# A list of five named buffers for the gathered expert rows, apart from the ring of the expert tiles

## The chip, the cores and the metric

One core of a Trainium2 chip runs the whole program. The metric is the device time of one execution in microseconds (us). The kernel is written in Python against a layer that keeps tiles in named buffers, puts in the semaphores between engines and sets each engine's order of instructions itself.

## The reference

The reference is two transformer blocks in float32 on one sequence of 256 tokens of width 2048. The first has a gated linear attention and a SwiGLU layer; the second a hybrid of sparse and stick-breaking attention, a memory attention, and a PEER layer, which is where the change lies. PEER keeps 16384 experts; expert e is a row `u[e]` and a row `v[e]` of 2048 numbers each. Each of 8 heads scores two sets of 128 keys against the token's query, keeps the best 16 pairs of keys (a pair names one expert) and softmaxes their scores to gates. Written out for one token x, with the 128 chosen experts e and their gates g:

```python
y = sum(g[e] * gelu(dot(u[e], x)) * v[e] for e in chosen)
out = rmsnorm(h + y, norm_final)
```

## The kernel before, in words

All activations lie with the width on the partitions. Up to the queries of PEER the kernel is a row of linear layers in three-pass float32, with weights loaded ahead, split into a high and a low part in buffers with the tags wh and wl, and multiplied on TensorE. The change touches nothing of that part but shares its buffers: `wtile(tag, i)` (line 188) gives the one buffer `tag` + `i`, a tile of 128 x 2048 floats, 1 MB. For the PEER layer there are wr0 to wr2, wh0 to wh2 and wl0 to wl2.

PEER is computed in two ways at once. For 160 of the 256 tokens (ND) the kernel multiplies with all 16384 experts and sets the gate of every expert that wasn't chosen to zero. For the other 96 tokens (SETS, 64 and 32) it fetches only the chosen rows.

The dense way reads the whole of u and v as 256 tiles of 1 MB, in the order of `expert_order` (line 77). They go through a ring of four buffers: wr0, wr1 and wr2, and ("wl", 2), which is appended at line 1307. `load_raw` (line 1035) takes a free slot and issues the next tile's load on SP (line 1041); `raw_weight` (line 1045) gives the slot of the last used tile back, loads ahead, and hands out the next tile. So SP is up to three tiles ahead of TensorE. `u_pair` (line 1071) takes two tiles of u and makes 256 hidden units for 160 tokens; between the pairs of the first part `gates` (line 1361) builds the dense gates with matmuls of one-hot rows that VectorE writes in `gates_rows` (line 1351). The loop at line 1392 takes the tiles of v.

The sparse way gathers. One gather fetches 128 rows of 2048 numbers, 1 MB, with an indirect DMA that POOL issues (line 1130). There are 192: 96 of u (64 for the first set, 32 for the second), then 96 of v. Gathered rows of u are multiplied and summed by VectorE at line 1142 into `hs`, rows of v are multiplied by `hs` and added to `hn` at line 1150. `gathered_steps` (line 1135) starts the first NG = 5 gathers; each step then uses one gather's rows and starts the gather five places on. The steps are paced by the ring: `raw_weight` adds 0.83 to a credit for each tile and takes a step for each whole one, and each gather waits for the matmul that was written last before it (line 1132). So there are about 83 gathers for 100 tiles, until all 192 are through.

Which buffer a gather uses is decided in `gather` (line 1126). Python reads `n % NG // 2` from the left, as (n % NG) // 2, while the tag alternates with n:

```python
g = fetched[n] = wtile(("wh", "wl")[n % 2], n % NG // 2, F32R).bitcast(F32)
```

For n from 0 to 9 that is wh0, wl0, wh1, wl1, wh2, wl0, wh0, wl1, wh1, wl2, and then from the start.

The layer underneath lets an instruction that reuses a buffer wait until the buffer's last user is done, and may place it later in its engine's order than the code does. An engine and SP's queue take their instructions in order.

Of the kernel before, what the change touches and what calls it, by code (L numbers as in the profile page):

```python
# [9 lines left out]
F32 = mybir.dt.float32  # L10
F32R = mybir.dt.float32r
# [21 lines left out]
LAG = 4  # L33
RATE = 3
PER = 1
NG = 5
SHARE = 5 / 8


# [42 lines left out]
def build(tc, a, out, dbg=None):  # L82
# [4 lines left out]
    with es:  # L87
# [100 lines left out]
        def wtile(tag, i, dt=F32):  # L188
            pool = wp if i < 2 else st["ext"]
            return pool.tile([P, 2048], dt, name=tag, tag=f"{tag}{i}", bufs=1)  # L190
# [21 lines left out]
        def weight(kt, n, hold=False):  # L212

            if not hold:
                w_free.extend(i for i in st["held"] if i < st["nw"])
                st["held"] = []
            load_ahead()
            w, h, l, i = ready.pop(0)
            st["held"].append(i)
            assert w == kt * n, (w, kt, n)  # L220
            v = lambda t: t[:, :w].rearrange("p (k n) -> p k n", n=n)
            return v(h), v(l)
# [105 lines left out]
        with ExitStack() as e1:  # L328
# [22 lines left out]
            with ExitStack() as e2:  # L351
# [145 lines left out]
                wh, wl = weight(KT, 16)  # L497
# [87 lines left out]
        with ExitStack() as e1:  # L585
# [18 lines left out]
            with ExitStack() as e2:  # L604
# [183 lines left out]
                wh, wl = weight(KT, 24)  # L788
# [154 lines left out]
        with ExitStack() as e1:  # L943
# [43 lines left out]
            for j in range(8):  # L987
                mt = mp.tile([P, 2, T], F32, name="mt2", tag="mt2")
                nc.sync.dma_start(mt, a["memT"][:, 2 * j:2 * j + 2])
                for i in range(2):  # L990
                    k = 2 * j + i
                    g = gains[:, 4, k:k + 1]
# [15 lines left out]
            for n4 in range(4):  # L1008
                wh, wl = weight(16, P)
# [15 lines left out]
        with ExitStack() as e1:  # L1025
# [98 lines left out]
            fetched = {}  # L1124

            def gather(n):
                if n < len(plan):
                    t, d, m = plan[n]
                    g = fetched[n] = wtile(("wh", "wl")[n % 2], n % NG // 2, F32R).bitcast(F32)
                    ins = nc.gpsimd.indirect_dma_start(g, None, a[t], bass.IndirectOffsetOnAxis(ap=d["ix"][:, m:m + 1], axis=0))  # L1130

                    tc.add_manual_dep(ins.ins, last_pe[0], mybir.DependencyInfo(
                        mybir.DependencyClass.Sync, mybir.DependencyReason.DATA), reason="pace")

            def gathered_steps():
                for n in range(NG):
                    gather(n)
                yield True
                for n, (t, d, m) in enumerate(plan):
                    g, h = fetched.pop(n), d["hs"]  # L1140
                    if t == "u_rows":
                        nc.vector.tensor_tensor_reduce(out=g, in0=g, in1=d["hn"], scale=1.0, scalar=0.0, op0=ALU.mult, op1=ALU.add,  # L1142
                                                       accum_out=h[:, m:m + 1])
                        if m == d["w"] - 1:
                            nc.scalar.activation(h, h, AF.Gelu_apprx_tanh)
                            nc.vector.tensor_tensor(h, h, d["gs"], ALU.mult)
                    elif m == 0:
                        nc.vector.tensor_scalar(d["y"], g, h[:, 0:1], None, ALU.mult)
                    else:
                        nc.vector.scalar_tensor_tensor(d["y"], g, h[:, m:m + 1], d["y"], ALU.mult, ALU.add)  # L1150
                        d["done"] = m == d["w"] - 1
                    gather(n + NG)
                    yield True
# [363 lines left out]
```

## Time and profile before

| | us |
|---|---|
| median of 2 runs | 3147.11 (3143.66 to 3150.56) |
| the profiled execution | 3146.22 |
| its span, first to last instruction | 3144.1 |
| TensorE (PE) busy in it | 3006.3 |
| VectorE (DVE) busy | 1713.8 |

The span is what the profile covers; the rest of the profiled execution lies around it. "PE" is TensorE's matmuls, "POOL" GpSimd, "SPq" the queue of SP. "PEclk" is the granted clock of TensorE as a share of its full speed, "DMA share" the mean busy share of the core's 16 DMA engines. In a row of a wait, "A <- B" says that A waited and that B ended the wait. A name such as wl stands for all buffers of that tag. A busy TensorE isn't one at its peak, since matmuls overlap.

### The profile page before, as it was taken

Reading aid. Unit: us, or ns where it says so; the run is one execution under the profiler, and the core shown is the slowest. Engines: PE = TensorE matmul, PEld = TensorE weight load, DVE = VectorE, ACT = ScalarE, POOL = GpSimd, SP = SyncE. Lnnn points to the kernel's source line nnn. Section 1 sums busy time; section 2 is a strip of 40 time slices with the busy share of each in tenths; the row PEclk is TensorE's granted clock in tenths of the full one; section 3 lists DMA queues with packets and bytes.
Section 4 is the critical chain, followed back from the end, with each engine's and each line's share of the span. In section 5 each row is a group of like instructions: output and inputs, shape, how many; then the busy total and the mean of one; then the engine's idle time right before and its main releaser. Section 6 shows DMA issues by size and latency. Waiting matters only on the chain.

```text
span 3144.1 us, 52115 instructions
## 1 busy us (share of the span) xinstructions
PE 3006.3 (96%) x22786; PEld 2938.4 (93%) x22786; DVE 1713.8 (55%) x2300; ACT 870.3 (28%) x1074; POOL 538.8 (17%) x367
## 2 busy tenths in 40 slices
PE   8999999999999999999999999999989889989998
PEld 7989999999999999899998999998989889989988
DVE  6575665454545555455867885656544434344332
ACT  5335544333333444343655421111100000000001
POOL 1120012011020210000111531112222222332210
PEclk9999999999999999999999999999999989999999
DMA  5444455554555546545355559999999989999995
GB/s 191 170 147 150 160 206 183 176 200 165 200 176 197 188 161 218 184 160 177 132 184 180 198 189 405 394 356 355 378 346 399 383 328 397 401 386 400 385 378 188
DMA packets 128351, 799.50 MB, mean 254 GB/s; under 512 B 18595, under 2 KB 25676, under 8 KB 39260
## 3 DMA queue, kind: packets, MB, share of 16 engines
q1 hardware_dynamic: 99548, 593.43, 51.8%
q0 software_dynamic: 27648, 201.34, 16.0%
q8 instruction: 178, 2.92, 0.4%
q10 hardware_dynamic: 928, 1.41, 0.2%
q14 instruction: 49, 0.40, 0.0%
HBM read 790.51 MB, written 5.78 MB: 253 GB/s over the span
## 4 chain that ended last, share of the span: by engine, by line
PE 78%; DMA 10%; DVE 6%; issue 4%; POOL 1%; ACT 1%; SPq 0%; ACTq 0%; POOLq 0%; DVEq 0%
PE lin L104 72%; PE att L104 5%; DMA wl<-in_peer_v 2%; DMA wl<-in_v_rows,ix 2%; DMA wl<-in_peer_u 2%; DMA wr<-in_peer_u 1%; DMA wh<-in_v_rows,ix 1%; DMA wr<-in_peer_v 1%; DVE wl L174 1%; DVE hn L1150 1%; DVE pair L277 0%; PE att L107 0%; ACT wh L170 0%; DVE wl L1142 0%; DVE s L1221 0%
## 5 line engine op out<-in xcount | busy, mean ns | idle before, releaser
L104 PE MATMUL lin<-pair,wh 128*128 128x256 f32 x5632 | 1013.0, 282 | 15.3 <-ACT pair L276 7.9
L104 PEld LDWEIGHTS lin<-pair,wh 128*128 128x128 f32 x5632 | 869.1, 190 | 21.2 <-DVE pair L277 9.9
L174 DVE TENSOR_TENSOR wl<-wr,wh 128x2048 fp32r<-128x2048 f32 (+3 forms) x316 | 658.2, 2084 | 422.3 <-ACT wh L170 422.2
L104 PE MATMUL lin<-pair,wl 128*128 128x256 f32 (+1 forms) x3200 | 852.2, 286 | 33.7 <-DMA wl<-in_peer_v 28.1
L170 ACT ACTIVATE wh<-wr 128x2048 fp32r<-128x2048 f32 (+2 forms) x316 | 557.2, 1764 | 814.9 <-PE lin L104 730.2
L104 PEld LDWEIGHTS lin<-pair,wl 128*128 128x128 f32 x3200 | 591.4, 191 | 35.5 <-DMA wl<-in_peer_v 29.1
L104 PE MATMUL lin<-xn,wr 128*128 128x160 f32 x3072 | 427.1, 299 | 3.1 <-DMA wr<-in_peer_u 2.9
L104 PEld LDWEIGHTS lin<-xn,wr 128*128 128x128 f32 x3072 | 419.3, 190 | 4.2 <-issue 2.7
L567 POOL TENSOR_TENSOR hv<-sg,gu 128x256 f32<-128x256 f32 x44 | 101.9, 2315 | 598.4 <-ACT sg L565 598.4
L104 PE MATMUL lin<-hh,wh 128*128 128x256 f32 x704 | 199.6, 284 | 2.1 <-ACT hh L170 2.1
L104 PE MATMUL lin<-xn,wl 128*128 128x160 f32 x1024 | 159.8, 318 | 43.3 <-DMA wl<-in_peer_u 43.2
L1150 DVE SCALAR_TENSOR_TENSOR hn<-wh,hs,hn 128x2048 f32<-128x2048 f32 x46 | 108.1, 2351 | 169.1 <-DMA wh<-in_v_rows,ix 168.9
L104 PE MATMUL lin<-hl,wh 128*128 128x256 f32 x704 | 199.6, 284 | 0.3
L1150 DVE SCALAR_TENSOR_TENSOR hn<-wl,hs,hn 128x2048 f32<-128x2048 f32 x48 | 112.9, 2351 | 159.1 <-DMA wl<-in_v_rows,ix 158.5
L104 PE MATMUL lin<-hh,wl 128*128 128x256 f32 x704 | 199.2, 283 | 0.0
L104 PEld LDWEIGHTS lin<-xn,wl 128*128 128x128 f32 x1024 | 154.8, 206 | 45.9 <-DMA wl<-in_peer_u 45.9
L104 PE MATMUL lin<-pair,wr 128*128 128x160 f32 x1216 | 170.8, 299 | 3.7 <-DMA wr<-in_peer_v 3.6
L104 PEld LDWEIGHTS lin<-pair,wr 128*128 128x128 f32 x1216 | 166.7, 190 | 5.1 <-DMA wr<-in_peer_v 4.3
L104 PE MATMUL lin<-hid,wr 128*128 128x160 f32 x1216 | 170.6, 299 | 0.3 <-DMA wr<-in_peer_v 0.2
L104 PEld LDWEIGHTS lin<-hid,wr 128*128 128x128 f32 x1216 | 166.8, 190 | 0.8 <-DMA wr<-in_peer_v 0.8
L1185 ACT ACTIVATE acc<-xs 128x192 f32<-128x192 f32 x1 | 0.4, 362 | 579.5 <-DVE xs L1171 579.5
L1142 DVE CUSTOM_DVE_ANT_0 wh<-wh,hn 128x2048 f32<-128x2048 f32 x48 | 109.9, 2289 | 90.6 <-DMA wh<-in_u_rows,ix 90.6
(339 smaller groups left out, 4078.7 us busy)
## 6 DMA issues: line engine op xcount, KB each, us to landing
wr<-in_peer_u SPq DMA_DIRECT2D x96, 1024.0 KB, 9.5
wr<-in_peer_v SPq DMA_DIRECT2D x96, 1024.0 KB, 10.9
wr<-in_w_gu SPq DMA_DIRECT2D x88, 1024.0 KB, 4.9
wr<-in_w_dn SPq DMA_DIRECT2D x64, 704.0 KB, 4.1
wr<-in_w_in SPq DMA_DIRECT2D x32, 1024.0 KB, 4.9
wl<-in_peer_u SPq DMA_DIRECT2D x32, 1024.0 KB, 9.6
wl<-in_peer_v SPq DMA_DIRECT2D x32, 1024.0 KB, 9.3
wr<-in_w_v SPq DMA_DIRECT2D x16, 1024.0 KB, 4.9
```

Of the source, the lines that this page charges most:

```text
L104: pin(nc.tensor.matmul(ps, l, r, start=start, stop=stop, **kw))
L170: nc.scalar.activation(h, src, AF.Copy)
L174: eng.tensor_tensor(l[:, lo:hi], src[:, lo:hi], h.bitcast(F32)[:, lo:hi], ALU.subtract)
L567: nc.gpsimd.tensor_tensor(hv, sg, gu[:, 1], ALU.mult)
L1142: nc.vector.tensor_tensor_reduce(out=g, in0=g, in1=d["hn"], scale=1.0, scalar=0.0, op0=ALU.mult, op1=ALU.add, accum_out=h[:, m:m + 1])
L1150: nc.vector.scalar_tensor_tensor(d["y"], g, h[:, m:m + 1], d["y"], ALU.mult, ALU.add)
L1185: nc.scalar.activation(sq, src, AF.Square)
```

## The change

The buffers of the gathers are written down in a list, and gather n takes the n-th of them in turn. NG keeps its value of 5. Nothing else is changed; every line from 37 on has a number that is higher by one.

```diff
-NG = 5
+ROWS = [("wh", 0), ("wl", 0), ("wh", 1), ("wl", 1), ("wh", 2)]
+NG = len(ROWS)
...
-                    g = fetched[n] = wtile(("wh", "wl")[n % 2], n % NG // 2, F32R).bitcast(F32)
+                    g = fetched[n] = wtile(*ROWS[n % NG], F32R).bitcast(F32)
```

The first place is POOL's order at the gathers around the stretch of time that the timeline below shows. The name of a tile is its tag and a number that tells one use of a buffer from another; what stands in brackets are the semaphores that the row waits for: PE, DVE, those of loads that SP issued (DMAHW) and of gathers (DMASW). Before:

```order
L1130 DMA wh_22427<-in_v_rows,ix0_16752 128x2048 [waits DMASW5_49,PE_49]
L1130 DMA wl_22466<-in_v_rows,ix0_16752 128x2048 [waits DMASW1_49,DVE_49,PE_49]
L1130 DMA wh_22487<-in_v_rows,ix0_16752 128x2048 [waits DMASW6_49,DMASW0_49,PE_49]
L1130 DMA wh_22529<-in_v_rows,ix0_16752 128x2048 [waits DMASW4_49,DVE_49,PE_49]
L1130 DMA wl_22508<-in_v_rows,ix0_16752 128x2048 [waits DMAHW4_49,DMAHW0_49,PE_49]
L1130 DMA wl_22550<-in_v_rows,ix0_16752 128x2048 [waits DMASW3_49]
L1130 DMA wh_22589<-in_v_rows,ix0_16752 128x2048 [waits DMASW2_49,DMASW6_49,DVE_49,PE_49]
```

After:

```order
L1131 DMA wl_22427<-in_v_rows,ix0_16752 128x2048 [waits DMASW7_49,DVE_49,PE_49]
L1131 DMA wh_22466<-in_v_rows,ix0_16752 128x2048 [waits DMASW0_49,DVE_49,PE_49]
L1131 DMA wl_22487<-in_v_rows,ix0_16752 128x2048 [waits DMASW1_49,DVE_49,PE_49]
L1131 DMA wh_22508<-in_v_rows,ix0_16752 128x2048 [waits DMASW2_49,DVE_49,PE_49]
L1131 DMA wh_22529<-in_v_rows,ix0_16752 128x2048 [waits DMASW3_49,DVE_49,PE_49]
L1131 DMA wl_22550<-in_v_rows,ix0_16752 128x2048 [waits DMASW4_49,DVE_49,PE_49]
L1131 DMA wh_22589<-in_v_rows,ix0_16752 128x2048 [waits DMASW5_49,DVE_49,PE_49]
```

The gather wl_22508, which is one with n % 10 = 9, stood behind wh_22529 and waited for a load of the ring (DMAHW); it is wh_22508 now, stands ahead of wh_22529, and waits for VectorE's use of the buffer five gathers ago.

The second place is SP's order between the last tiles of u and the first of v. `wl` and `wr` are loads into the ring, xn is the activations of the 160 tokens that are read back. Before:

```order
L1041 DMA wr_22020<-in_peer_v 128x2048 [waits DMAHW6_49,PE_49]
L1398 DMA xn_22050<-xD_16746 128x16x160 [waits PE_49]
L1041 DMA wr_22076<-in_peer_v 128x2048 [waits DMAHW0_49,PE_49]
L1041 DMA wr_22094<-in_peer_v 128x2048 [waits DMAHW1_49,PE_49]
L1041 DMA wr_22115<-in_peer_v 128x2048 [waits DMAHW2_49,PE_49]
L1041 DMA wl_22053<-in_peer_v 128x2048 [waits DMAHW7_49,DMASW4_49,DVE_49]
L1041 DMA wl_22136<-in_peer_v 128x2048 [waits DMAHW7_49,PE_49]
```

After:

```order
L1042 DMA wr_22020<-in_peer_v 128x2048 [waits DMAHW6_49,PE_49]
L1042 DMA wl_22053<-in_peer_v 128x2048 [waits DMAHW7_49,PE_49]
L1399 DMA xn_22050<-xD_16746 128x16x160
L1042 DMA wr_22076<-in_peer_v 128x2048 [waits DMAHW0_49,PE_49]
L1042 DMA wr_22094<-in_peer_v 128x2048 [waits DMAHW1_49,PE_49]
L1042 DMA wr_22115<-in_peer_v 128x2048 [waits DMAHW2_49,PE_49]
L1042 DMA wl_22136<-in_peer_v 128x2048 [waits DMAHW3_49,PE_49]
```

The load wl_22053 stood behind three loads into wr and the one of xn, and waited for VectorE and a gather; it stands ahead of them and waits for TensorE and an older load. Before, 19 loads of the ring into wl waited for VectorE, and none does after. TensorE's rows are the same in both, in the same order.

## Rows read from the trace of the kernel before

**Rows 1.** The page: the span, and what the DMA moved in its 40 slices
```profile
span 3144.1 us, 52115 instructions
...
GB/s 191 170 147 150 160 206 183 176 200 165 200 176 197 188 161 218 184 160 177 132 184 180 198 189 405 394 356 355 378 346 399 383 328 397 401 386 400 385 378 188
```

**Rows 2.** TensorE's waits for wl, by stretch as in rows 5: total us, times, longest
```profile
PE lin L104 <- DMA wl<-in_peer_u: 20.8, 6, 6.3
...
PE lin L104 <- DMA wl<-in_peer_u: 22.3, 3, 12.6
...
PE lin L104 <- DMA wl<-in_peer_v: 51.6, 10, 17.6
```

**Rows 3.** Waits of SP, which issues the ring's loads, from 1880 us on
```profile
SPq L1041 <- DVE hs L1142: 131.9, 8, 19.7
SPq L1041 <- DMA wl<-in_v_rows,ix: 110.9, 9, 13.9
```

**Rows 4.** Timeline, 2618 to 2660 us: start, us, engine, line, [idle before]
```profile
2620.63 4.51 PE L104 MATMUL lin<-hid,wl 128*128 128x160 f32 x32
...
2625.41 2.69 POOL L1130 DMA_INDIRECT wl<-in_v_rows,ix  x1 [2.30 <-PE lin L104]
...
2634.32 2.35 DVE L1150 SCALAR_TENSOR_TENSOR hn<-wl,hs,hn 128x2048 f32<-128x2048 f32 x1 [7.03 <-DMA wl<-in_v_rows,ix]
...
2636.75 0.33 SPq L1041 DMA_DIRECT2D wl<-in_peer_v  x1
2637.17 1.92 SPq L1041 DMA_DIRECT2D wr<-in_peer_v  x3
...
2644.09 7.08 PE L104 MATMUL lin<-hid,wl 128*128 128x160 f32 x32 [5.92 <-DMA wl<-in_peer_v]
```

**Rows 5.** Three stretches and the end: us, engines' busy time, PEclk, DMA share, GB/s
```profile
1945.00:2325.00 380.00, 355.63 (x2596) 353.78 (x2594) 235.13 (x502) 42.46 (x147) 76.27 (x60) 0.97 0.95 370
2325.00:2505.00 180.00, 160.46 (x1132) 159.82 (x1132) 66.67 (x69) 7.55 (x18) 37.32 (x29) 0.93 0.94 376
2505.00:3060.00 555.00, 499.28 (x3526) 494.75 (x3525) 224.00 (x107) 0.00 (x0) 142.38 (x89) 0.95 0.96 384
3060.00:3120.00 60.00, 60.00 (x448) 60.00 (x448) 12.98 (x37) 6.68 (x16) 0.00 (x0) 1.00 0.72 246
```

**Rows 6.** Matmuls that read wl, by stretch: busy us (count)
```profile
1945.00:2325.00 380.00, 90.06 (x576) 0.97 0.95 370
2325.00:2505.00 180.00, 47.01 (x288) 0.93 0.94 376
2505.00:3060.00 555.00, 143.09 (x895) 0.95 0.96 384
```

**Rows 7.** Matmuls that read wr, by stretch
```profile
1945.00:2325.00 380.00, 241.18 (x1732) 0.97 0.95 370
2325.00:2505.00 180.00, 115.81 (x844) 0.93 0.94 376
2505.00:3060.00 555.00, 361.29 (x2615) 0.95 0.96 384
```

**Rows 8.** Windows with little or no stall of TensorE
```profile
2000.00:2040.00 40.00, 39.68 (x298) 39.43 (x298) 26.52 (x56) 5.32 (x20) 8.06 (x7) 1.00 1.00 411
2300.00:2320.00 20.00, 20.00 (x152) 20.00 (x151) 11.93 (x22) 2.05 (x7) 6.26 (x4) 1.00 0.96 338
2880.00:2920.00 40.00, 40.00 (x294) 40.00 (x294) 19.77 (x15) 0.00 (x0) 6.51 (x6) 0.98 1.01 419
2960.00:2980.00 20.00, 20.00 (x149) 20.00 (x149) 7.42 (x5) 0.00 (x0) 2.19 (x3) 1.00 1.01 417
```

**Rows 9.** Timeline of SP in the last of these windows
```profile
2966.41 9.02 SPq L1041 DMA_DIRECT2D wr<-in_peer_v  x3
```

**Rows 10.** The gates' matmuls in the first stretch: busy, mean ns | idle before
```profile
L104 PE MATMUL att<-Bg,sq 128*128 128x128 f32 x288 | 38.0, 275 | 0.0
```

**Rows 11.** One reduction of gathered rows, the timeline at 2104 us
```profile
2104.20 2.28 DVE L1142 CUSTOM_DVE_ANT_0 wh<-wh,hn 128x2048 f32<-128x2048 f32 x1
```

## The prediction

> **What bounds the kernel now.** I read the page first, for its slices, then the waits of TensorE and of SP in the part where the slices change, then the timeline around one wait, and last the windows of that part. The slices show two kernels in one: the DMA moves 130 to 220 GB/s up to slice 24 and 328 to 405 GB/s from there on, about 1886 us to the end [rows 1]. That is the part in which 256 expert tiles of 1 MB go through the four ring buffers (wr0 to wr2 and wl2) while 192 gathers of 1 MB each go through the buffers that the change names. The change touches nothing ahead of it.
>
> There TensorE waits for loads into wl, and for hardly anything else: 20.8 us in 6 waits in the first of three stretches, 22.3 us in 3 in the second, 51.6 us in 10 in the third [rows 2], 94.7 us in 19 waits. Of the ring's four buffers only wl2 has that tag, and 19 is a number that the code gives: the buffer of gather n is chosen by n % 5 and by the parity of n apart, so n = 9, 19, ... 189 falls on ("wl", 2), the ring's own. The timeline shows one of the 19 [rows 4]. TensorE reads the tile in wl2 from 2620.63 to 2625.1; at 2625.41 POOL starts a gather into that buffer instead of SP a load; VectorE uses the rows from 2634.32 to 2636.67; at 2636.75 SP issues the load, and right behind it, from 2637.17, three loads into wr that had stood behind it in SP's order. The tile is used at 2644.09, after 5.92 us without work. So a buffer is gone from the ring for 11.6 us, and SP's whole queue is held. SP's own waits say the same: 131.9 us for what VectorE does with gathered rows of the first half and 110.9 us for gathers into wl in the second [rows 3], none of which a ring of tiles should need.
>
> A stall costs twice. After it the granted clock is down: it is 0.93 to 0.97 in the three stretches that hold the stalls and 1.00 at the end, between the two levels of 1.2 and 2.4 GHz [rows 5]. By matmul: those that read wl, the ones that come after a stall, are busy 90.06, 47.01 and 143.09 us for 576, 288 and 895 [rows 6]; those that read wr 241.18, 115.81 and 361.29 us for 1732, 844 and 2615, that is 0.1393, 0.1372 and 0.1382 us each [rows 7]. At that price the wl ones would take 80.2, 39.5 and 123.7 us. The surplus is 9.9, 7.5 and 19.4 us, 36.8 in all.
>
> **What the change removes.** All 19 visits of gathers to wl2. The five buffers are then used in strict turn, none of them the ring's. In the order of SP the loads into wl lose their waits on VectorE and on a gather; TensorE's order is the same row for row. The load of xn from xD, which SP issued three tiles ahead of such a held load, stands behind it now; its bytes are the same and are in the sums below. With the stalls go 94.7 us, and with them the 36.8 us of slow clock: 131.5 us at most, 30.7, 29.8 and 71.0 us by stretch.
>
> **What it adds.** No instruction. Per ten gathers one more goes into wh, one less into wl; the count and the bytes stay, 1 MB each. Two edits I cost at nothing. POOL's gathers stand in plain turn now, where the tenth was overtaken by the one after it. POOL is busy 76 of 380 us in the first stretch and 142 of 555 in the third [rows 5] and waits the rest of its time, which hides a change of place; without that cover a gather would be late by the 2.69 us that one took to issue [rows 4], 19 times, 51 us at the most. VectorE's reductions of a tenth and its neighbour trade places, 9 times in the first half, and some pass the gate rows that TensorE's gate matmuls wait for. One takes 2.28 us [rows 11], so 9 of them cost 20.5 us if nothing covered them. The cover is that the 288 gate matmuls have 0.0 us of idle time ahead of them now [rows 10]; for the same reason nothing can be gained there. I take 0 for both, the value of the rows that stand nearest, and keep +51 and +20.5 for the range.
>
> **What is late next.** The transfers. Removing stalls doesn't remove bytes: the three stretches move 370, 376 and 384 GB/s [rows 5], 140.6, 67.7 and 213.1 MB. Without the stalls TensorE would be through in 349.3, 150.2 and 484.0 us, and that needs 403, 451 and 440 GB/s. Where TensorE doesn't wait and the DMA is full (share 1.00 to 1.01) the rows have 411, 419 and 417 GB/s [rows 8]. So the first stretch, where gate matmuls lie between the tiles, stays bound by TensorE; the second and third become bound by the DMA. There SP should always have three loads out beside a gather, so nothing leaves the DMA idle, and short waits for wr and wl spread evenly take the place of the 19 long ones. A slow clock costs nothing extra while the data is what is late.
>
> Of the ceilings I take 411 GB/s, the lowest of the three full ones, since no window as long as a stretch is full. First stretch: 380 to 349.3, less 30.7 us. Second: 67.7 MB / 411 = 164.7, less 15.3. Third: 213.1 / 411 = 518.5, less 36.5. Sum 82.5 us. At 419 it is 30.7 + 18.4 + 46.4 = 95.5. The profiled execution took 3146.2 us, 2.1 of it outside the span, and stands 0.9 under the median of 3147.1 of the runs shown: 3146.2 less 82.5 is 3063.7, say 3064 us.
>
> The Trainium skill sets the ceiling otherwise: its page DMA: Bandwidth & Descriptors, section "Where 436 GB/s comes from", gives 435.2 GB/s for the ports into SBUF and about 358 GB/s for one core's half of the HBM, of which the lower would bind a load. By the 358 nothing could be gained, and the trace doesn't agree, with 419 GB/s over 40 us [rows 8]. By the 435.2, as an estimate, the stretches would take 349.3, 155.6 and 489.7 us and the kernel 3026 us; no row here reaches it.
>
> **The rivals.** *The whole 131.5 us comes*, 3015 us. For it: gathers may lag and finish in the last stretch, where the DMA moves only 246 GB/s for 60 us [rows 5]. Against it: only five can lag, and 440 GB/s is above every row shown.
>
> *The DMA is fuller than its GB/s say.* Its share is 0.95, 0.94 and 0.96 already [rows 5], 1.01 when full [rows 8]. If the busy time per byte stays as it is, the stretches shrink only to 357.4, 167.5 and 527.5 us, 62.6 in all: 3084 us. For it: a share of 0.96 with only 338 GB/s exists [rows 8]. Against it: that window ends just ahead of the longest wait of the second stretch, with loads held back.
>
> *It doesn't do what it says*: the stall moves on, because the ring is only three tiles ahead of TensorE and each load shares the DMA with a gather. Then waits for wr take over most of the 131.5 us, and it ends within 30 us of now, about 3130. Against it: in the windows at 417 and 419 GB/s TensorE is busy all the time [rows 8], with both kinds of transfer under way.
>
> *Slower*: it is the hold that lets SP issue three or four loads at once [rows 4], and the DMA may be full only because of that. Issued one by one, loads beside gathers could run at the 338 GB/s of 2300 us [rows 8]: 416, 200 and 630 us for the three stretches, 131 more, 3277 us. It decides from 378 GB/s down, the mean of now (421.4 MB in 1115 us). Against it: from 2966.41 SP issues its three loads spread over 9.02 us [rows 9], one per tile, and that window moves 417 GB/s.
>
> **How the numbers follow.** The forecast (3045 to 3078 us) has 0.55, the whole gain or most of it 0.13, the DMA's share 0.18, no effect or a small one 0.09, slower 0.05. A measurement of this kernel can tell about 2%, 63 us, so the line lies at 3084: the forecast, the whole gain and half of the share's case lie below it, 0.77; 0.18 within; 0.05 above. The range leaves out the far part of the whole gain, and of no effect, and the slower case: 3035 to 3098 us.
>
> **What would show it.** Right: no long wait of TensorE for wl, no wait of SP on VectorE for a tile of the ring; 3 stretches of about 349, 165 and 518 us; GB/s near 403, 411 and 411 and the share near 1.0; PEclk at 1.00 in the first stretch; what waits remain are short, on wr and wl alike, in the peer_v part above all. Wrong: waits on wr that add up to more than 60 us; GB/s that stays under 390 in the third stretch with a share of 1.0; a gate matmul that waits for VectorE.

## The result and the profile after

The changed kernel takes 3050.62 us (median of 2 runs, 3050.34 to 3050.91) against 3147.11: a ratio of 0.9693, with a 95% interval from 0.9648 to 0.9739. It is faster by 96.5 us; 3064 was forecast, in a range from 3035 to 3098. The profiled execution took 3050.34 us with a span of 3048.2, 95.9 us less than before. Times are medians; one of the five executions of the run with one place of ten below took 4263.11 us at a granted clock of 0.654, and the ratios leave it out.

The page of the changed kernel: its span, and by 40 slices the granted clock of TensorE in tenths (9 is 90% or more) and the DMA's GB/s.

```profile
span 3048.2 us, 52095 instructions
...
PEclk9999999999999999999999999999999999999999
...
GB/s 193 170 148 153 152 207 183 168 205 168 199 187 165 207 164 207 194 180 158 166 135 208 195 159 274 419 416 400 403 401 413 419 407 419 418 417 418 417 400 182
```

The last 16 slices are the part in question, from 1829 us on. Before, they swung between 328 and 405 GB/s [rows 1]; now, but for the first and the last, they lie between 400 and 419. The slices ahead of it are much as they were.

TensorE's waits for loads from 1880 us to the end (total us, times, longest):

```profile
PE lin L105 <- DMA wr<-in_peer_v: 16.7, 27, 5.6
PE lin L105 <- DMA wl<-in_peer_v: 3.9, 8, 1.3
PE lin L105 <- DMA wr<-in_peer_u: 2.4, 5, 1.1
PE lin L105 <- DMA wl<-in_peer_u: 1.5, 5, 0.3
```

The 94.7 us in 19 waits for wl [rows 2] are gone. There are 45 short ones instead, 24.5 us in all, one in five of their time for wl, and most of it in the peer_v part. One of 5.6 us stands out; it comes back below.

SP's waits in the same part:

```profile
SPq L1042 <- PE lin L105: 848.3, 199, 8.9
SPq L1042 <- PE att L105: 173.8, 41, 4.7
```

SP waits for TensorE, 240 times, as a ring of tiles should: a tile must be used before its buffer is loaded again. Its 131.9 us for VectorE and 110.9 us for gathers [rows 3] are gone.

The timeline of the changed kernel at two places (start, us, engine, line, operation, count, and in brackets the idle time before it with what ended it):

```profile
2441.66 0.33 SPq L1042 DMA_DIRECT2D wl<-in_peer_v  x1
...
2442.03 0.54 SPq L1399 DMA_DIRECT2D xn<-xD  x1
...
2446.66 10.25 SPq L1042 DMA_DIRECT2D wr<-in_peer_v  x3
...
2466.49 15.19 PE L105 MATMUL lin<-pair,wr 128*128 128x160 f32 x96 [5.59 <-DMA wr<-in_peer_v]
...
2577.35 13.20 PE L105 MATMUL lin<-hid,wr 128*128 128x160 f32 x96
2577.55 0.33 SPq L1042 DMA_DIRECT2D wl<-in_peer_v  x1
2577.79 0.94 POOL L1131 DMA_INDIRECT wh<-in_v_rows,ix  x1 [3.41 <-PE lin L105]
...
2581.89 9.02 SPq L1042 DMA_DIRECT2D wr<-in_peer_v  x3
...
2590.39 4.51 PE L105 MATMUL lin<-hid,wl 128*128 128x160 f32 x32
```

The rows from 2577.35 on are a plain turn of the ring, to be read against the hold of [rows 4]: TensorE goes on to the next tile, SP loads the free wl buffer 0.20 us later, a gather starts 0.24 us behind that, three loads into wr follow one by one, and when TensorE is back at wl at 2590.39 there is no idle time in front of the row. The first four rows are the one wait of 5.59 us: between two loads of the ring SP issues xn, 1.3 MB in pieces of 640 bytes, and the tile of 2466.49 is late. SP took 8.83 us to issue the first of the three loads that follow, where a row of one load has 0.33. The window from 2450 us in the next table is what the DMA does then.

The stretches in the changed kernel (us, busy time of PE, PEld, DVE, ACT, POOL with their counts, PEclk, DMA share, GB/s):

```profile
1943.00:2290.00 347.00, 346.51 (x2596) 345.55 (x2595) 231.63 (x500) 42.52 (x147) 63.96 (x59) 1.00 1.00 406
2290.00:2456.00 166.00, 160.74 (x1154) 156.90 (x1153) 74.46 (x74) 7.67 (x18) 34.76 (x30) 1.00 1.02 415
2456.00:2960.00 504.00, 484.33 (x3481) 475.12 (x3480) 216.79 (x104) 0.00 (x0) 106.80 (x89) 0.99 1.01 417
2450.00:2460.00 10.00, 9.61 (x71) 9.37 (x70) 4.70 (x2) 0.00 (x0) 4.04 (x2) 1.00 1.06 377
```

They answer to [rows 5], where the GB/s were 370, 376 and 384 and the clock 0.97, 0.93 and 0.95. The first stretch is TensorE's, busy 346.51 of 347 us. The other two are the DMA's, at 415 and 417 GB/s with a share of 1.01 to 1.02. While xn is read, a share of 1.06 goes with only 377 GB/s.

Matmuls that read wl in the three stretches, then those that read wr (length, busy us, count):

```profile
1943.00:2290.00 347.00, 81.39 (x576) 1.00 1.00 406
2290.00:2456.00 166.00, 41.01 (x288) 1.00 1.02 415
2456.00:2960.00 504.00, 123.45 (x868) 0.99 1.01 417
```

```profile
1943.00:2290.00 347.00, 241.54 (x1732) 1.00 1.00 406
2290.00:2456.00 166.00, 121.20 (x866) 1.00 1.02 415
2456.00:2960.00 504.00, 365.15 (x2597) 0.99 1.01 417
```

Per matmul wl takes 0.1413, 0.1424 and 0.1422 us, wr 0.1395, 0.1400 and 0.1406. Worked out as for [rows 6, 7], the surplus of the wl matmuls is 1.1 + 0.7 + 1.4 = 3.2 us, where it was 36.8. Not all of that fall is gain, since the price of a wr matmul rose in the second and third stretch, from 0.1372 to 0.1400 and from 0.1382 to 0.1406 us, 8.7 us for all of them.

How much each stretch gave is read between the same places of the program, the ends of four tiles. TensorE's timeline of the kernel before at these places:

```profile
1940.90 4.51 PE L104 MATMUL lin<-xn,wr 128*128 128x160 f32 x32
...
2317.70 4.51 PE L104 MATMUL lin<-xn,wr 128*128 128x160 f32 x32
...
2497.80 10.21 PE L104 MATMUL lin<-pair,wr 128*128 128x160 f32 x74
...
3127.86 4.51 PE L104 MATMUL lin<-hid,wl 128*128 128x160 f32 x32
```

And of the changed kernel:

```profile
1939.27 4.51 PE L105 MATMUL lin<-xn,wr 128*128 128x160 f32 x32
...
2285.95 4.51 PE L105 MATMUL lin<-xn,wr 128*128 128x160 f32 x32
...
2451.94 4.61 PE L105 MATMUL lin<-pair,wr 128*128 128x160 f32 x32 [0.39 <-DMA wr<-in_peer_v]
...
3031.43 4.51 PE L105 MATMUL lin<-hid,wl 128*128 128x160 f32 x32
```

The ends are 1945.41, 2322.21, 2508.01 and 3132.37 us before, and 1943.78, 2290.46, 2456.55 and 3035.94 after. So the first stretch went from 376.8 to 346.7 us (30.1 less), the second from 185.8 to 166.1 (19.7 less), the third, with the end, from 624.4 to 579.4 (45.0 less). These are 94.8 of the 95.9 us.

### The profile page after: what moved, and what is told of

Read it like the earlier page. It is cut to its first block, busy times and chain, and to the rows that moved or that the text cites. A ratio compares the mean times of both kernels' runs of the same rounds, so it can differ in the third digit from the quotient of the medians.

```text
span 3048.2 us, 52095 instructions
## 1 busy us (share of the span) xinstructions
PE 2987.1 (98%) x22786; PEld 2911.7 (96%) x22786; DVE 1710.6 (56%) x2300; ACT 870.4 (29%) x1074; POOL 494.5 (16%) x367
## 4 chain that ended last, share of the span: by engine, by line
PE 82%; DMA 11%; DVE 5%; ACT 1%; issue 0%; POOL 0%; ACTq 0%; DVEq 0%; POOLq 0%; SPq 0%
PE lin L105 75%; PE att L105 6%; DMA wr<-in_peer_v 4%; DMA wr<-in_peer_u 4%; DMA wl<-in_peer_v 2%; DVE wl L175 1%; DMA wl<-in_peer_u 1%; DVE pair L278 0%; PE att L108 0%; ACT wh L171 0%; DVE s L1222 0%; DVE e L1276 0%; DVE ti L1225 0%; DVE ti L1224 0%; POOL hv L568 0%
## 5 line engine op out<-in xcount | busy, mean ns | idle before, releaser
L1151 DVE SCALAR_TENSOR_TENSOR hn<-wh,hs,hn 128x2048 f32<-128x2048 f32 x56 | 131.7, 2352 | 156.8 <-DMA wh<-in_v_rows,ix 156.7
L105 PE MATMUL lin<-xn,wl 128*128 128x160 f32 x1024 | 145.1, 300 | 1.9 <-DMA wl<-in_peer_u 1.5
L1143 DVE CUSTOM_DVE_ANT_0 wh<-wh,hn 128x2048 f32<-128x2048 f32 x58 | 132.7, 2288 | 24.9 <-PE att L108 17.7
L105 PE MATMUL lin<-wh,pair 128*128 128x512 f32 x448 | 146.0, 399 | 0.0
L105 PEld LDWEIGHTS lin<-xn,wl 128*128 128x128 f32 x1024 | 140.6, 190 | 3.8 <-DMA wl<-in_peer_u 3.8
```

The source lines that it names most:

```text
L105: pin(nc.tensor.matmul(ps, l, r, start=start, stop=stop, **kw))
```

## The experiments

The theory: a gather in wl2 holds one of the ring's four buffers, TensorE stalls and its clock falls; without that, bytes bound the second and third stretch. The first two runs look at the hold, the next ones at what is late after it.

**One place of ten.** The order of before, with only the entry of the ring's buffer replaced:

```diff
-g = fetched[n] = wtile(("wh", "wl")[n % 2], n % NG // 2, F32R).bitcast(F32)
+TEN = [("wh", 0), ("wl", 0), ("wh", 1), ("wl", 1), ("wh", 2), ("wl", 0), ("wh", 0), ("wl", 1), ("wh", 1), ("wh", 2)]
+g = fetched[n] = wtile(*TEN[n % 10], F32R).bitcast(F32)
```

> The order of buffers of the kernel before, with one entry of ten changed: gather n = 9, 19, ... goes to wh2 instead of wl2. Theory (the visit to the ring's buffer is all of it): 3050 us, within 6 of the changed kernel. Rival (the strict turn of five is worth something, because in this order a buffer comes back after four gathers in half of the cases and the gather has to wait for one reduction more): each such wait some 2.3 us and more in 38 places, 3080 to 3130 us.

Measured: 3052.18 us (median of five; the four that the ratio goes by lie from 3048.67 to 3054.01), a ratio of 0.9705 (0.9673 to 0.9738). That is the whole gain of the change within its interval. The visit to the ring's buffer is what cost; the strict turn of the other buffers is worth nothing that can be measured.

**A visit in five.** The list's last entry becomes the ring's buffer, so 38 gathers go there:

```diff
-ROWS = [("wh", 0), ("wl", 0), ("wh", 1), ("wl", 1), ("wh", 2)]
+ROWS = [("wh", 0), ("wl", 0), ("wh", 1), ("wl", 1), ("wl", 2)]
```

> The changed kernel with wl2 in place of wh2 in the list: every fifth gather visits the ring, 38 in all instead of 19. Theory (each visit holds the ring and SP's queue): 19 visits cost 96 us between the two kernels, so 38 cost about 190, 3240 us, and TensorE waits for wl some 38 times. Rival (a second visit hides in the shadow of the first, or the 19 were costly only since the tenth gather was overtaken by the eleventh): below 3180 us.

Measured: 3196.95 us, a ratio to the kernel before of 1.0166 (1.0111 to 1.0222). It lies between the theory's 3240 and the rival's bound of 3180 us. TensorE's waits for loads into wl from 1880 us on:

```profile
PE lin L105 <- DMA wl<-in_peer_v: 65.6, 19, 17.5
PE lin L105 <- DMA wl<-in_peer_u: 63.5, 19, 14.7
```

And SP's, those behind a gather or its use:

```profile
SPq L1042 <- DVE hs L1143: 301.9, 19, 19.4
SPq L1042 <- DMA wl<-in_v_rows,ix: 212.6, 16, 16.4
```

There are exactly 38 waits of TensorE for wl, one for each visit, and SP waits for VectorE and for gathers again. So the count holds. The size doesn't: a wait is 3.4 us in the mean (129.1 / 38) instead of 5.0, and the 19 further visits cost 55 us (3196.95 less 3142.34, the kernel before on that chip) where the first 19 cost 96. The expected price per visit was too high for the second half of them. Why a second visit in a turn is cheaper wasn't settled.

**A deeper ring.** Five ring buffers, four for the gathers:

```diff
-ROWS = [("wh", 0), ("wl", 0), ("wh", 1), ("wl", 1), ("wh", 2)]
+ROWS = [("wh", 0), ("wl", 0), ("wh", 1), ("wl", 1)]
...
-slots.append(("wl", 2))
+slots.extend([("wl", 2), ("wh", 2)])
```

> The changed kernel with wh2 given to the ring: five ring buffers, four for gathers. Theory (from the end of the gates on the DMA's 419 GB/s are the bound): 3050 us within 8, GB/s at 419 as before, since a deeper ring brings no bytes faster; the 5.6 us wait at the change from u to v may go. Rival (the ring's depth of three tiles ahead is the bound, the waits for wr come from the latency of single loads): the 30 us of waits that are left go, 3015 to 3025 us. Other rival (the gathers need five buffers): over 3065 us.

Measured: 3045.58 us, 0.9686 (0.9653 to 0.9719), not apart from the changed kernel. Its window of the third stretch, columns as above (the second has 415 GB/s at a share of 1.02):

```profile
2456.00:2960.00 504.00, 482.49 (x3472) 473.96 (x3471) 216.92 (x104) 0.00 (x0) 117.37 (x89) 0.99 1.01 417
```

The GB/s are those of the changed kernel. One more tile of lead doesn't make bytes come sooner, and the waits for loads add up to 25.5 us against 24.5, so it isn't the depth of the ring that is short.

**Half of the gathers of v left out.** Each second gather of v isn't issued, and the step that would use it reads its neighbour's rows again. That leaves out 48 gathers, some 50 MB; all instructions on VectorE and TensorE stay.

```diff
+if t == "v_rows" and m % 2:
+    fetched[n] = fetched[n - 1]
+    return
...
-g, h = fetched.pop(n), d["hs"]
+g, h = fetched[n], d["hs"]
```

> The changed kernel that gathers only every second of the 96 blocks of rows of v; each reduction in between reads its neighbour's rows again, so half of the sparse tokens' sum over v is left out and replaced. Reductions, ring and order stay. Theory (the bytes of ring and gathers together at 419 GB/s bound the v part): the need falls to 1.42 x 1.0486 MB in 4.36 us, 340 GB/s, so the waits for wr and wl in the v part go and it takes TensorE's time: 128 tiles x 4.355 us = 557 us and 4 us of transposes, instead of 594 us: 33 us less at most, 3018 us, 3023 if the wait at the change from u to v stays. Rival (the ring's depth and each load's latency make the waits): less than 10 us, 3041 us or more.

Measured: 3018.31 us, 0.9595 (0.9573 to 0.9616), 32 us under the changed kernel. Its third stretch up to 2940 us:

```profile
2456.00:2940.00 484.00, 484.00 (x3568) 484.00 (x3568) 217.12 (x104) 0.00 (x0) 66.17 (x44) 1.00 0.92 340
```

And what TensorE waits for from 1880 us on:

```profile
PE lin L105 <- DMA wr<-in_peer_u: 4.5, 9, 1.0
PE lin L105 <- DMA wl<-in_peer_u: 1.6, 6, 0.3
```

TensorE is busy 484.00 of 484.00 us, the DMA moves 340 GB/s, and no wait for a load from peer_v is left. A matmul takes 484.00 / 3568 = 0.1357 us there against 484.33 / 3481 = 0.1391 in the changed kernel, so 3481 of them give back 12 us; the waits for peer_v gave 20.6. Together these are the 32 us, but for 2.2 us more of waits for peer_u. Only 48 transfers were taken out, and with them POOL's issues (POOL was busy 106.80 of 504 us there) and the waits for their rows; every other instruction is the same. TensorE's waits were for loads of the ring, which this run leaves as they are, so it is the bytes beside them that decide the last part of the changed kernel. This run carries most of the weight.

**Another pace.** If bytes bound the later stretches and TensorE the first, fewer gathers per tile should thin out the former. Three runs change the pace of steps (0.83 of a step per tile): 0.78 throughout, 0.81 throughout, and 0.9 up to the end of the gates with 0.795 after them.

```diff
-ring["rate"] = 0.83
+ring["rate"] = 0.78
```

> The changed kernel with 0.78 steps of gathers for each tile instead of 0.83: same bytes, spread over some 15 tiles more, into the part that had 230 to 270 GB/s. Theory (DMA bound): a tile with its gathers takes 1.78 x 1.0486 MB / 419 = 4.455 us instead of 4.58 in the second and third stretch, about 145 tiles, so 18 us less: 3032 us, within 6. Rival (the depth of the ring or the order of loads is the bound, not the bytes): 3045 to 3052 us.

> The changed kernel with 0.81 steps for each tile. With 0.78 the stalls of TensorE went but the sparse tokens were finished only after the last tile, 17 us later than in the changed kernel. In the changed kernel that finish is over 23 us before the last tile of v is through, so 5 tiles more of gathers still fit. Theory (bytes bound the second and third stretch): 145 tiles at 1.81 x 1.0486 MB / 419 = 4.53 us instead of 4.58 us, 7 us less: 3043 us, within 4. Rival (not the bytes): 3050 us as in the changed kernel.

```diff
-ring["rate"] = 0.83
+ring["rate"] = 0.9
...
+ring["rate"] = 0.795
```

> The changed kernel with a rate of 0.9 up to the end of the gates and 0.795 from there, so that the last gather falls at the same tile as in the changed kernel. Theory: the first stretch stays bound by TensorE (it needs 415 GB/s), the tiles after it cost 1.795 x 1.0486 / 419 = 4.49 us instead of 4.58, 145 of them: 13 us less, 3038 us, within 5, and the waits of TensorE fall from 26 to about 13 us. Rival (the waits stem from latency, not from bytes): 3050 us, the same waits.

Measured: 3054.28 (0.971, 0.9678 to 0.9742), 3053.80 (0.9699, 0.9678 to 0.972) and 3047.62 us (0.968, 0.9658 to 0.9701). All three fell short, by 22, 11 and 10 us, and none is apart from the changed kernel. Some of the reasons show. At 0.81 TensorE has these rows in the last part, of its waits and of its timeline:

```profile
PE lin L105 <- DMA wr<-in_peer_v: 16.0, 16, 9.3
...
3028.81 0.36 PE L105 MATMUL att<-acc,ones 128*128 128x96 f32 x2
...
3039.42 0.87 PE L105 MATMUL att<-acc,ones 128*128 128x160 f32 x2 [5.43 <-DVE acc L1190]
```

The first row is fewer waits (16 instead of 27), as bytes that are spread thinner should give, but not less time, since the one behind xn has grown from 5.6 to 9.3 us. The other two are the end of the program. With a slower pace the 96 sparse tokens are finished later: TensorE's matmul for their norm stands at 3028.81, just ahead of the last tile, where the changed kernel has it at 3004.68, seven tiles ahead of the end of its tiles. VectorE's work on them then falls together with its sum `acc` for the 160 dense tokens, and TensorE waits 5.4 us for that sum; in the changed kernel it doesn't. At 0.78 the sparse tokens' matmul comes only after the last tile, at 3058.07 where the last tile ends at 3051.47. With two rates the first stretch, up to 2290 us, looks like this:

```profile
1943.00:2290.00 347.00, 345.05 (x2569) 342.13 (x2568) 243.99 (x515) 43.04 (x150) 72.65 (x65) 1.00 1.01 418
```

At 0.9 the DMA is as full there as in the later stretches, 418 GB/s against 406, and TensorE gets through 27 matmuls fewer. The first stretch had room for 12 GB/s more in 347 us, about 4 MB. I had counted on more of it. But 27 matmuls are only some 4 us, and TensorE's waits for loads did fall with two rates, from 24.5 to 20.0 us; for the rest of the 10 us that are missing no run shows the cause.

**Two rates and the deeper ring** together (both diffs above):

> The two rates together with five ring buffers and four for the gathers. Theory: the two gains add, 13 and 5 us: 3033 us, within 5. Rival (with four buffers the gathers come too late for the higher rate in the first stretch): 3045 us or more.

Measured: 3048.97 us, 0.9684 (0.9663 to 0.9705). The two gains don't add. One reason shows in the trace: of 27.9 us of waits for loads 13.97 are a single one, at 2480.24, for a tile whose load stands behind xn; SP took 15.83 us to issue that load. With the deeper ring alone the same wait is 8.7 us, in the changed kernel 5.6.

**xn in eight pieces.** The load behind the wait of 5.59 us, cut up and issued behind every second tile:

```diff
-nc.sync.dma_start(xr[1], xD[:, :, NS:T])
+if dq == 0 and c < 16 and c % 2 == 0:
+    tc.keep_in_program_order(nc.sync.dma_start(xr[1][:, c:c + 2], xD[:, c:c + 2, NS:T]))
```

> The changed kernel with the load of xn (1280 KB in rows of 640 bytes, issued by SP between two loads of the ring) cut into 8 loads of 160 KB, one behind every second tile of v. Theory (it is what makes the wait of 5.6 us at 2461 us): the wait goes, the clock stays up there, 5 to 8 us less: 3044 us. Rival (the wait is part of the shortage of bytes and comes back as short waits in the tiles after it): 3050 us as in the changed kernel.

Measured: 3048.61 us, 0.9696 (0.9674 to 0.9719). TensorE's waits for wr from peer_v:

```profile
PE lin L105 <- DMA wr<-in_peer_v: 15.5, 31, 1.8
```

The longest is 1.8 us instead of 5.6, and their sum is 15.5 instead of 16.7; all waits for loads are 25.5 us instead of 24.5. The single wait was where the shortage of bytes showed first, not a cost of its own: cut it up, and the same bytes are missed elsewhere. The time lies between the theory's 3044 and the rival's 3050, nearer to the rival.

**Pieces and two rates** (0.88 and 0.8):

> The changed kernel with the eight loads of xn and rates of 0.88 up to the end of the gates and 0.8 from there. Theory: 5 to 8 us from xn and some 5 us from the rates: 3038 us, within 5. Rival (both are the same shortage of bytes): 3046 us, as the two rates alone.

Measured: 3043.07 us, 0.9679 (0.9657 to 0.97), the lowest of those that leave nothing out, between the theory's 3038 and the rival's 3046, with an interval that overlaps the change's. No version beats the changed kernel clearly.

**The held load in a queue of its own.** This one is made on the kernel before. The prediction counted it among the costs of a hold that SP's whole queue is held; here the ring's loads into wl are issued by ScalarE's queue in the v part, so that those into wr no longer stand behind them:

```diff
+queue = nc.scalar if slot[0] == "wl" and ring["next"] >= P else nc.sync
-tc.keep_in_program_order(nc.sync.dma_start(t, raws[ring["next"]]))
+tc.keep_in_program_order(queue.dma_start(t, raws[ring["next"]]))
```

> The kernel before, with the loads of tiles of v into wl issued by ACT instead of SP, so that a held load no longer stands in front of three loads into wr. ACT has nothing else to do in most of the v part. It asks which half of a hold costs: the tile that is late itself, or the queue behind it. If it is the tile itself: TensorE still waits about 50 us for wl in the v part, and the time stays within 10 us of the kernel before. If it is SP's queue: the waits in the v part fall by half or more and 20 to 45 us go.

Measured: 3187.29 us, 1.0136 (1.0113 to 1.0159) times the kernel before on that chip (3143.43). TensorE's waits for wl:

```profile
PE lin L104 <- DMA wl<-in_peer_v: 93.8, 10, 12.6
PE lin L104 <- DMA wl<-in_peer_u: 41.5, 10, 11.1
```

In the u part, where the queue is the same, they are as before (41.5 us in 10 against 20.8 + 22.3 in 9). In the v part they are 93.8 us in 10 against 51.6 in 10 [rows 2]. The window from 2505 us:

```profile
2505.00:3100.00 595.00, 505.61 (x3526) 503.47 (x3527) 218.77 (x105) 0.00 (x0) 118.37 (x88) 0.92 0.90 354
```

And the timeline of one of these holds:

```profile
2683.27 1.21 POOL L1131 DMA_INDIRECT wl<-in_v_rows,ix  x1 [3.41 <-PE lin L104]
2687.38 9.02 SPq L1042 DMA_DIRECT2D wr<-in_peer_v  x3
...
2691.79 2.35 DVE L1151 SCALAR_TENSOR_TENSOR hn<-wl,hs,hn 128x2048 f32<-128x2048 f32 x1 [8.12 <-DMA wl<-in_v_rows,ix]
...
2694.22 0.34 ACTq L1042 DMA_DIRECT2D wl<-in_peer_v  x1
...
2705.62 6.62 PE L104 MATMUL lin<-pair,wl 128*128 128x160 f32 x31 [9.58 <-DMA wl<-in_peer_v]
```

The gather into the ring's buffer starts at 2683.27 and VectorE has its rows at 2691.79, 8.5 us later, as before (8.9 us in [rows 4]). VectorE is through at 2694.14, ScalarE's queue issues the load at 2694.22, and TensorE has it at 2705.62. That is 11.4 us against 7.3 from 2636.75 to 2644.09 in [rows 4], where the load was the first of four and the three into wr came behind it. Here SP issues its three one by one from 2687.38 on, ahead of the one that is needed first. From 2694 to 2706 us the DMA moves 406 GB/s at a share of 1.01, so it is not idle while the held load is late: it moves other bytes, some 4.6 MB in the 11.4 us, where it moved 2.8 MB in the 7.3 us before. That the three loads share the DMA with the held one is the likely reason; that a load from ScalarE's queue is served more slowly by itself isn't ruled out. The 4.1 us more in this hold are about the 4.2 us more of the mean wait (9.4 against 5.2), and the stretch falls to 354 GB/s.

**The tenth gather late.** The last run puts POOL's order of before back into the changed kernel: every tenth gather is started a step later, behind the one after it. Its buffer stays apart from the ring.

```diff
-gather(n + NG)
+if (n + NG) % 10 != 9:
+    gather(n + NG)
+if (n + NG) % 10 == 0:
+    gather(n + NG - 1)
```

> The changed kernel, in which every tenth gather (n % 10 = 9) is started one step later, behind the one after it, as in POOL's order before; its buffer is wh2 now and not the ring's. TensorE's order is the same. The prediction cost the move of these gathers in POOL's order at nothing, between 0 and 51 us (19 times the 2.69 us that an issue took). If the 0 is right, this run takes the changed kernel's 3051 us within 8 us, the rows come about 5 us later but still before VectorE needs them, and TensorE waits for loads some 25 us from 1880 us on, none of it for wl alone. The rival: POOL's order was part of the gain. Then a gather that is late by a step of about 5 us makes VectorE late, the pace and the ends of the sparse tokens with it, and the run takes 3070 to 3100 us.

Measured: 3055.92 us, 0.9698 (0.9678 to 0.9719): 5.3 us more than the changed kernel, within the 8 of the expectation and not apart by the intervals. TensorE's longest groups of waits from 1880 us on:

```profile
PE lin L105 <- DMA wr<-in_peer_v: 14.8, 22, 7.4
PE lin L105 <- DMA wr<-in_peer_u: 8.1, 6, 5.1
```

All of its waits for loads are 27.1 us, where the changed kernel has 24.5. So POOL's order by itself was no part of the gain, or a small one.

## Why the prediction was right

**What the change removes: right.** 19 holds, one in ten gathers, each with a wait of TensorE. All are gone, the run with one place of ten shows that nothing else in the list matters, and the one with a visit in five that each visit makes one wait. The slow clock behind a stall is real: the surplus of the wl matmuls fell from 36.8 to 3.2 us with no matmul changed. As a price it was somewhat too high, since 8.7 us came back on the wr matmuls. The granted clock of the first stretch is 1.00.

**The terms at nothing: right for POOL's order, within 5 us; VectorE's not tried alone.** For POOL's order the bounds were 0 and 51 us and 0 was taken; with the old order put back it measures 5.3 us, which two such intervals don't tell from 0. For the gates' matmuls, which VectorE's places could have made late, the changed kernel's row is that of [rows 10] again, with no idle time before them (busy us, mean ns | idle):

```profile
L105 PE MATMUL att<-Bg,sq 128*128 128x128 f32 x288 | 38.0, 275 | 0.0
```

**What is late next: right in kind.** The first stretch is TensorE's; it gave 30.1 us where 30.7 were worked out. The second and third are the DMA's: the share is 1.01 to 1.02, the waits are short and lie on wr and wl, 19.1 and 5.4 us, about as their tiles do, three to one; with half of the gathers of v left out they vanish in the v part, and the kernel takes what TensorE needs. Of the 131.5 us that the stalls and the slow clock took, 95.9 came. The rest is put down to the transfers; of it, 24.5 us of waits for loads (6.1 us of them, for wr, were there before) and the 8.7 us of dearer wr matmuls can be seen.

**The term that was mis-sized: the ceiling.** I took 411 GB/s, the lowest of the three full windows of before [rows 8], "since no window as long as a stretch is full". The stretches ran at 415 and 417. So the second gave 19.7 us where 15.3 were taken, the third 45.0 where 36.5 were; at 419 GB/s, the prediction's other bound, they would have been 18.4 and 46.4, and the sum 95.5 against 95.9 measured. With the measured 415 and 417 the same sum gives 30.7 + 16.9 + 44.0 = 91.6, so some 4 us of the 95.9 are not the ceiling's, and what they are isn't shown. The window at 411 was no ceiling of the DMA: it lies at 2000 us, in the first stretch, where TensorE sets the pace. There the changed kernel moves 406 GB/s with TensorE busy 346.51 of 347 us, and with more gathers per tile (the rate of 0.9) it moves 418. The two windows of the third stretch, at 419 and 417, were the ones to take.

**A reason that was wrong beside the sum.** "SP's whole queue is held" was told as part of what a hold costs. The run with ScalarE's queue shows the opposite: with SP's queue released, the waits for wl in the v part nearly doubled. The likely reason is that the loads into wr, while they stood behind the held one, kept the DMA free for it. No term rested on it, since the stalls were counted from TensorE's waits.

**The rivals.** That the whole 131.5 us comes (3015 us) fails on the DMA, which was at 417 GB/s of the 440 that it needs; with half of v's gathers left out, which lowers the need, the time is 3018. That a share of 0.96 leaves no room (3084 us) fails: the same share of 1.01 now goes with 417 GB/s instead of the 404 (213.1 MB in 527.5 us) of this reckoning. That the waits move to wr (3130 us) is there in kind, but at 19.1 us for wr, not the better part of 131.5. The slower one, that loads one at a time run at 338 GB/s, fails on the same 417, with the loads issued one per tile [rows 9], as at 2581.89 above.

**What stayed open.** The lower cost of a second hold in a turn. And whether an order exists that comes nearer to the 3018 us of the run with fewer bytes: the seven versions that tried ended between 3043 and 3054 us. And what a slower pace of gathers in the third stretch would give, if nothing came late at the end of the program.

## What to carry to other kernels

A buffer that two streams share ties the lag of the slower to the faster: here each gather in the ring's buffer cost 5 us of waiting and 2 us of slower clock, of which 5 could be had back. Count such visits from the code, price them from the waits of the engine that is late, and then ask in each stretch by itself what the bytes allow without them; what the DMA moved in windows without stalls was the right ceiling, as long as the windows are those of the same stretch: a window in which TensorE sets the pace shows what was asked of the DMA and not what it can do. Before a held load is moved to a queue of its own, look at what the hold keeps back: it may be traffic that the held load is better off without.

## What the runs showed that was not expected

One core kept 417 GB/s over 504 us, in direct loads and gathers of 1 MB side by side; the windows of before had left open whether that lasts. The DMA's busy share says little about headroom: 0.95 at 370 GB/s with stalls, 1.01 at 417 without, 1.06 at 377 while rows of 640 bytes were read, and 0.90 at 354 with the held loads in a second queue. And of two ways to issue the same loads, the one with a blocked queue was the faster by 1.4%.
